# Summing two halves of each attention head in the store, moving two loads to another queue, and scaling the last rows in place

## The chip, the cores and the metric

The kernel is written in a tile framework for one Trainium2 chip and runs on one core of it. The core has TensorE for matrix products, VectorE (DVE), ScalarE (ACT) and GpSimd (POOL) for elementwise work, and SyncE (SP), which here only issues transfers. SP, ScalarE and GpSimd each have a queue for transfers (DMA) between the chip's memory (DRAM) and the on-chip buffer. The metric is the time of one execution on the device, in microseconds; the time given is the median of several runs.

The author writes the instructions in a program order and names tiles out of pools with a fixed number of buffers. A planner then decides in which order each engine takes its own instructions and which buffer a tile gets, and adds the waits on semaphores that the data need. On the chip each engine works through its list strictly in order: an instruction whose inputs aren't there holds back all that stand behind it on that engine, issues of transfers included.

## What is computed

One decoder block over 1024 tokens of width 1024, in float32: a norm, one wide projection, two token mixers, a gated merge, an output projection, and a gated FFN with a short convolution, then a last norm.

```python
xn = rms_norm(h, norm_mix_g)
proj = xn @ w_in                       # q, k, v of both mixers, gates
o_sb  = stick_breaking_attention(...)  # 8 heads of 64, causal
o_gla = gla_chunked(...)               # 4 heads, gated linear attention in chunks
y = sigmoid(gate_sb + b0) * (o_sb @ w_branch_sb) + sigmoid(gate_gla + b1) * (o_gla @ w_branch_gla)
h = h + y @ w_out
h = h + conv_ffn(rms_norm(h, norm_ffn_g))
return rms_norm(h, norm_final_g)
```

The change concerns the way `o_sb` takes from the attention to its product with `w_branch_sb`, the loads of keys for the gated linear attention ("the gated branch"), and the very last rows that are written.

## The kernel before

**Split products.** A float32 value is used on TensorE as a high and a low part: `split(h, l, src)` (L121) rounds `src` into `h` on ScalarE (L122, a cast) and subtracts on VectorE (L113) to get `l`. `mac` (L199) multiplies high by high, high by low and low by high into one bank of PSUM; its matmuls are those of line 205.

**Attention** (`attend`, L883). The eight heads are taken in four pairs `j`; in each pair `tp` counts four steps of two blocks of 128 queries, and `e` the two heads. For every chunk of up to four blocks of keys, `weigh` (L821) computes scores on TensorE (L828), a sigmoid on ScalarE (L830) and a scan on VectorE (L833, L835) into a tile `ke` of the pool `t2`. Up to `AHEAD` = 6 chunks are in flight; then `turn_weights` transposes them on TensorE (L842) and splits them. When both blocks of a step are turned, `gather` (L865) multiplies them with the values (L871). Keys and queries of the next pair come through the POOL queue (`keys`, `queries`, L737).

The values stand in a tile as 64 columns of high parts beside 64 columns of low parts. So the bank that `gather` fills has 128 rows: rows 0 to 63 hold the head's result from the high parts, rows 64 to 127 that from the low parts, and the head's output is the sum of the two. `gather` adds a bias (L877, ScalarE) into a tile `o` of pool `t2` and stores each half of `o` on its own, through SP (L879): the first to rows `head * 64` on of the scratch matrix `osb_d`, the second to the same rows further down by 512.

`heads(th)` (L847) brings this back for one half `th` of the sequence: for each of four groups of 128 rows it loads the two matrices' parts into two `t2` tiles (SP, L855), adds them (VectorE, L119) and splits the sum (L122, L113) into `ob[th]`, from which `branch(0, ...)` (L1072) multiplies with `w_branch_sb`. `heads(0)` is stepped along inside `attend` once head 7 has finished step `tp` = 1; `heads(1)` follows at the start of the gated branch (L1161).

**Gates beside it.** Pieces of the merge-gate projection (`gates`, L686) are mixed into attention as filler for TensorE; they end in a sigmoid (L719) and a store in ScalarE's queue (L720).

**After attention.** `branch(0, ...)` first loads four slabs of `w_branch_sb` (L181; two of the loads through POOL, L1077); then `fetch_rest` (L956) loads the two tiles `kt` of keys for the gated branch through POOL (L962). The gated branch (`gated`, L1047) starts with `states`, whose matmuls (L970) read `kt`; TensorE alternates between it and `branch(0, ...)`. Its `out_pair` copies a bank on ScalarE (L998), masks it on POOL (L999) and multiplies (L1007).

**Pools.** `t2` has 11 buffers of 128x512, `t4` 14 of 128x1024, `t8` 16 of 128x2048, and there are 8 banks.

**The end.** The last phase of the FFN's product ends four times in `fourth_done` (L1417), for rows of the second half of the sequence: subtract the bank, square and sum, root and reciprocal, scale both halves of the row by the norm's factor and by `norm_final_g`. The scaled row is put into one of two `spare` tiles, which `third_done` (L1402) used before, and stored through POOL; the very last one goes out in two halves through SP and ScalarE.

Of the kernel before, what the change touches and what calls it, by code (L numbers as in the profile page):

```python
# [12 lines left out]
AF = mybir.ActivationFunctionType  # L13
ALU = mybir.AluOpType
# [3 lines left out]
P = 128  # L18
# [4 lines left out]
HALF = 512  # L23
# [45 lines left out]
def block_kernel(ctx: ExitStack, tc: tile.TileContext, x, norm_mix_g, w_in, b_gate, w_alpha_up, b_alpha,  # L69
                 gla_norm_g, w_branch_sb, w_branch_gla, w_out, norm_ffn_g, w_ffn_in, conv_w, conv_b,  # L70
                 w_ffn_out, norm_final_g, out):
    nc = tc.nc
    x, out = x[0], out[0]
# [6 lines left out]
    def nm(s):  # L80
        uid[0] += 1
        return f"{s}_{uid[0]}"
# [7 lines left out]
    def t8(dt=F32R):  # L90
        return sb.tile([P, 2 * D], dt, tag="t8", name=nm("t8"), bufs=16)

    def t4(dt=F32):
        return sb.tile([P, D], dt, tag="t4", name=nm("t4"), bufs=T4)

    def t2(dt=F32):
        return sb.tile([P, HALF], dt, tag="t2", name=nm("t2"), bufs=T2)

    def bank():
        return ps.tile([P, HALF], F32, tag="bank", name=nm("bank"), bufs=8)  # L100

    def dram(name, rows, cols, dt=F32):
        return dp.tile([rows, cols], dt, tag=name, name=name)

    def by(a, k):
        return a.rearrange("p (k c) -> p k c", k=k)

    def quarter():

        return [by(t8(), 4) for _ in range(2)]  # L110

    def sub(o, a, b):
        nc.vector.tensor_tensor(out=o, in0=a, in1=b, op=ALU.subtract)  # L113
# [4 lines left out]
    def add(o, a, b):  # L118
        nc.vector.tensor_tensor(out=o, in0=a, in1=b, op=ALU.add)  # L119

    def split(h, l, src):  # L121
        nc.scalar.copy(h, src)  # L122
        sub(l, src, h.bitcast(F32))
# [43 lines left out]
    qd_d, ki_d, kt_d = (dram(n, GH * GK, S) for n in ("qd_d", "ki_d", "kt_d"))  # L167
    gate_d, ga_d = dram("gate_d", 2 * D, S), dram("ga_d", 2 * RANK, S)
    osb_d = dram("osb_d", 2 * SBH * SBD, S)
# [388 lines left out]
    for half in range(2):  # L558
# [5 lines left out]
        o = t2()  # L564
# [162 lines left out]
    HALVES = slice(0, 64), slice(64, 128)  # L727
# [117 lines left out]
    ob, first_heads = [], []  # L845

    def heads(th):  # L847

        ob.append(quarter())
        asked, added = deque(), deque()  # L850
        for k in range(6):
            if k < 4:
                asked.append((t2(), t2()))
                for n, v in enumerate(asked[-1]):
                    nc.sync.dma_start(v, osb_d[n * HALF + k * P:n * HALF + (k + 1) * P, th * HALF:(th + 1) * HALF])  # L855
            yield
            if k > 1:
                split(*(a[:, k - 2] for a in ob[th]), added.popleft())
            if k in range(1, 5):
                a, b = asked.popleft()  # L860
                add(a, a, b)
                added.append(a)
            yield

    def gather(head, tp, ah, al):  # L865
        po = bank()
        nb = 2 * tp + 2
        for b in range(nb):
            c0 = 0 if b < nb - 1 else P
            for n, a in enumerate((ah, al)):  # L870
                nc.tensor.matmul(po[:, c0:2 * P], vt[b][:, head, :], a[b // 4][:, b % 4, c0:],  # L871
                                 start=(b == 0 and n == 0), stop=(b == nb - 1 and n == 1))
        o = t2()[:, 0:2 * P]
        for n in range(2):
            c = slice(n * P, (n + 1) * P)
            i = head * NT + 2 * tp + n
            nc.scalar.activation(o[:, c], po[:, c], AF.Identity, bias=vend[:, i:i + 1])  # L877
        for n, r in enumerate(HALVES):
            nc.sync.dma_start(osb_d[n * HALF + head * 64:n * HALF + (head + 1) * 64, tp * 2 * P:(tp + 1) * 2 * P], o[r])  # L879
        if head == SBH - 1 and tp == 1:  # L880
            first_heads.append(heads(0))

    def attend():  # L883
# [10 lines left out]
        for j in range(SBH // 2):  # L894
            t, nxt = nxt, []
            for tp in range(NT // 2):
# [5 lines left out]
                for e in range(2):  # L902
                    ng = (2 * tp + 2 + 3) // 4
                    ah, al = ([by(t4(F32R), 4) for _ in range(ng)] for _ in range(2))
                    for ii in range(2):
                        i = 2 * tp + ii
                        nb = i + 1
                        right = None
                        for b0, b1 in ([(0, nb)] if nb <= 4 else [(4, nb), (0, 4)]):
                            while len(todo) == AHEAD or sum(d[1] for d in todo) > BLOCKS:  # L910
                                if len(late) > LATE:
                                    gather(*late.popleft())
                                flush()
                            right = weigh(t, e, i, b0, b1, right)
                            if j == 0:
                                chunk += 1
                                if chunk in HOLD:
                                    hold(right)
                                if chunk == AGAIN:
                                    whole21()  # L920
                                if chunk >= 2:
                                    fill(gate_steps, MORE * (chunk < 8))
                                    value_blocks(2 * tp + 2)
                            g = b0 // 4
                            d = [a[g][:, 0:b1 - b0, ii * P:(ii + 1) * P] for a in (ah, al)]
                            end = (2 * j + e, tp, ah, al) if ii == 1 and b0 == 0 else None
                            todo.append((right, b1 - b0, *d, end))
                            for v in first_heads:
                                next(v, None)
                            yield b1 - b0  # L930
        while todo:
            flush()
            while late:
                gather(*late.popleft())
            for v in first_heads:
                next(v, None)
            yield 2
# [18 lines left out]
    def fetch_rest():  # L956

        small = [by(t2(), 4) for _ in range(2)]
        state.extend((v[:, 0], v[:, 1]) for v in small)
        for p in range(2):  # L960
            kt = t4()
            nc.gpsimd.dma_start(kt, kt_d[p * P:(p + 1) * P, :])  # L962
            gla[p] += by(kt, NT), by(t4(), NT)

    def states(p, n0, n1):
# [186 lines left out]
    first_branch = branch(0, ob, w_branch_sb)  # L1152
    fill(first_branch, 1)
    fetch_rest()
    fill(gate_steps, 128)
    xq.clear()
    og = [quarter() for _ in range(2)]
    n = 0
    for _ in gated():
        if n == HEADS_AT:  # L1160
            fill(heads(1), 12)  # L1161
        n += 1
        fill(first_branch, n % GLA[1] < GLA[0])
        pace(0)
# [119 lines left out]
    acts, hr = [], []  # L1284
# [44 lines left out]
    def row(i, j):  # L1329
        return hr[i][:, j * HALF:(j + 1) * HALF]  # L1330
# [57 lines left out]
    gfin = []  # L1388
# [26 lines left out]
            mul(row(4 + i, 1), row(4 + i, 1), gfin[0][:, HALF:])  # L1415

    def fourth_done(i, p4):  # L1417
        r = row(4 + i, 0)
        sub(r, r, p4)
        o = spare[i % 2]  # L1420
        a, b = ss[i]
        nc.scalar.activation(o[:, :HALF], r, AF.Square, accum_out=b)
        add(a, a, b)
        nc.scalar.activation(b, a, AF.Sqrt, bias=eps, scale=1.0 / D)
        nc.vector.reciprocal(a, b)
        nc.scalar.activation(o[:, HALF:], row(4 + i, 1), AF.Copy, scale=a)
        nc.vector.scalar_tensor_tensor(out=o[:, :HALF], in0=r, scalar=a, in1=gfin[0][:, :HALF],
                                       op0=ALU.mult, op1=ALU.mult)
        t = slice((4 + i) * P, (5 + i) * P)
        if i < 3:  # L1430
            nc.gpsimd.dma_start(out[t, :], o)
        else:
            nc.sync.dma_start(out[t, :HALF], o[:, :HALF])
            nc.scalar.dma_start(out[t, HALF:], o[:, HALF:])

    for n, _ in enumerate(jobs):
        if n == 0:
# [9 lines left out]
    spare = [t4() for _ in range(2)]  # L1447
    spare8 = by(t8(F32), 4)
    phase(first, 2, 0, first_done, residual)
    phase(second, 2, 0, second_done, last_norm)  # L1450
    phase(third, 2, TILED[0], third_done)
    phase(fourth, 1, TILED[1], fourth_done, squares)


# [25 lines left out]
```

## Time and profile before

| | |
|---|---|
| median of 3 runs | 1386.93 us (1386.27 to 1387.03) |
| the profiled execution, its own time | 1386.67 us |
| its span, first to last instruction | 1384.8 us |
| instructions | 18329 |
| mean granted TensorE clock | 0.997 |
| read from and written to DRAM | 160.28 MB, 66.45 MB |

The profile lists for each engine the time in which it worked, and for each group of instructions what ended the idle time ahead of it. A row names the line of the kernel, the engine, the operation, the tiles (output<-input) and their shapes. Many instructions come from helpers: L113 is any subtraction, L119 any addition, L122 any cast of a split, L205 any product by `mac`, L181 any load by `load`. Such lines are told apart by their place in time. In a timeline, rows are start, duration, engine, line, operation, and in brackets how long the engine stood idle before and what ended that; "SPq", "ACTq" and "POOL ... DMA_DIRECT2D" are issues of transfers. "To landing" is the time from the issue to the end of a transfer.

Attention lies at about 343 to 538 us of the span, the gated branch with `branch(0, ...)` at 538 to 600, and the last matmul ends at 1377.6.

### The profile page before, as it was taken

Reading aid. Unit: us, or ns where it says so; the run is one execution under the profiler, and the core shown is the slowest. Engines: PE = TensorE matmul, PEld = TensorE weight load, DVE = VectorE, ACT = ScalarE, POOL = GpSimd, SP = SyncE. Lnnn points to the kernel's source line nnn. Section 1 sums busy time; section 2 is a strip of 40 time slices with the busy share of each in tenths; the row PEclk is TensorE's granted clock in tenths of the full one; section 3 lists DMA queues with packets and bytes.
Section 4 is the critical chain, followed back from the end, with each engine's and each line's share of the span. In section 5 each row is a group of like instructions: output and inputs, shape, how many; then the busy total and the mean of one; then the engine's idle time right before and its main releaser. Section 6 shows DMA issues by size and latency. Waiting matters only on the chain.

```text
span 1384.8 us, 18329 instructions
## 1 busy us (share of the span) xinstructions
PE 1372.4 (99%) x6559; PEld 1138.8 (82%) x6559; DVE 1064.6 (77%) x1640; ACT 643.9 (46%) x1244; POOL 136.3 (10%) x233
## 2 busy tenths in 40 slices
PE   9999999999999999999999999999999999999997
PEld 6788888888888888888888788888888888888886
DVE  6388688874878877658348998998888977896765
ACT  7334445653766664724126443343333334454654
POOL 2002123101111002200000000000000000000000
PEclk9999999999999999999999999999999999999999
DMA  6335278448776567673325245554444537953332
GB/s 239 132 117 151 84 221 251 143 158 210 216 158 151 131 197 237 198 237 136 136 91 177 52 120 187 196 189 152 150 163 152 182 107 272 322 163 102 99 101 105
DMA packets 164108, 227.92 MB, mean 165 GB/s; under 512 B 10938, under 2 KB 105276, under 8 KB 163506
## 3 DMA queue, kind: packets, MB, share of 16 engines
q1 hardware_dynamic: 134944, 139.01, 33.0%
q0 software_dynamic: 22496, 73.73, 16.8%
q10 hardware_dynamic: 6578, 14.03, 2.7%
q8 instruction: 51, 0.84, 0.3%
q14 instruction: 39, 0.32, 0.1%
HBM read 160.28 MB, written 66.45 MB: 164 GB/s over the span
## 4 chain that ended last, share of the span: by engine, by line
PE 95%; DVE 3%; ACT 1%; issue 0%; DMA 0%; ACTq 0%; DVEq 0%
PE bank L205 58%; PE bank L1343 15%; PE bank L385 6%; PE bank L1210 6%; PE bank L871 3%; PE bank L828 2%; PE bank L842 2%; DVE t L113 2%; PE bank L494 1%; PE bank L340 1%; DVE t L119 1%; PE bank L562 1%; PE bank L1007 1%; PE bank L970 0%; PE bank L994 0%
## 5 line engine op out<-in xcount | busy, mean ns | idle before, releaser
L205 PE MATMUL bank<-t,t 128*128 128x512 f32 x3624 | 861.1, 393 | 0.9 <-DVE t L113 0.7
L205 PEld LDWEIGHTS bank<-t,t 128*128 128x128 f32 x3624 | 676.5, 188 | 143.1 <-DVE t L113 1.6
L113 DVE TENSOR_TENSOR t<-t,t 128x512 fp32r<-128x512 f32 (+3 forms) x655 | 434.6, 697 | 93.5 <-ACT t L122 87.2
L122 ACT CAST t<-t 128x512 fp32r<-128x512 f32 (+1 forms) x543 | 320.3, 627 | 325.4 <-DVE t L113 81.0
L119 DVE TENSOR_TENSOR t<-bank,t 128x512 f32<-128x512 f32 x266 | 179.3, 685 | 97.9 <-PE bank L205 54.9
L1343 PE MATMUL bank<-t,t 128*128 128x512 f32 x924 | 209.6, 389 | 0.0
L1343 PEld LDWEIGHTS bank<-t,t 128*128 128x128 f32 x924 | 173.5, 188 | 36.0
L113 DVE TENSOR_TENSOR t<-bank,t 128x512 fp32r<-128x512 f32 (+4 forms) x124 | 69.5, 574 | 27.5 <-ACT t L122 26.9
L1210 PE MATMUL bank<-t,t 128*128 128x512 f32 x384 | 88.8, 391 | 0.0
L1241 ACT ACTIVATE t<-t,vcol 128x1024 f32<-128x1024 f32 x22 | 27.4, 1245 | 127.5 <-DVE t L119 127.5
L113 DVE TENSOR_TENSOR t<-t 128x512 f32<-128x512 f32 x120 | 83.3, 701 | 4.1 <-DMA t<-in_w_ffn_in_dram 3.7
L1210 PEld LDWEIGHTS bank<-t,t 128*128 128x128 f32 x384 | 71.6, 188 | 14.6
L119 DVE TENSOR_TENSOR t<-t,t 128x512 f32<-128x512 f32 x115 | 75.5, 686 | 9.8 <-ACT t L628 8.6
L122 ACT CAST t<-bank 128x512 fp32r<-128x512 f32 (+3 forms) x120 | 60.3, 512 | 48.8 <-PE bank L842 26.8
L385 PE MATMUL bank<-t,t 128*128 128x512 f32 x336 | 77.9, 391 | 0.0
L385 PEld LDWEIGHTS bank<-t,t 128*128 128x128 f32 x336 | 62.7, 188 | 13.1 <-DVE t L113 0.2
L1243 DVE SCALAR_TENSOR_TENSOR t<-t,vcol,t 128x1023 f32<-128x1023 f32 (+1 forms) x44 | 56.3, 1279 | 14.1 <-ACT t L1241 13.9
L833 DVE TENSOR_TENSOR_SCAN t<-t,t 128x128 f32<-128x128 f32 (+1 forms) x64 | 51.6, 816 | 17.5 <-ACT t L830 17.2
L828 PE MATMUL bank<-t,t 128*128 128x128 f32 (+3 forms) x192 | 54.6, 369 | 0.0
L842 PE MATMUL bank<-ident,t 128*128 128x128 f32 x288 | 53.2, 273 | 0.0
L871 PE MATMUL bank<-t,t 128*128 128x256 f32 (+1 forms) x320 | 51.0, 276 | 1.2 <-ACT t L122 0.7
L830 ACT ACTIVATE t<-bank 128x128 f32<-128x128 f32 (+3 forms) x96 | 46.9, 507 | 7.2 <-DMA osb_d<-t 3.2
(164 smaller groups left out, 813.5 us busy)
## 6 DMA issues: line engine op xcount, KB each, us to landing
t<-in_w_ffn_in_dram SPq DMA_DIRECT2D x50, 512.0 KB, 5.1
t<-in_w_in_dram SPq DMA_DIRECT2D x43, 512.0 KB, 5.3
act_d<-t POOLq DMA_DIRECT2D x22, 512.0 KB, 5.8
t<-in_w_ffn_out_dram SPq DMA_DIRECT2D x22, 512.0 KB, 7.6
wsum_d<-t POOLq DMA_DIRECT2D x22, 512.0 KB, 4.5
t<-act_d SPq DMA_DIRECT2D x22, 512.0 KB, 5.9
t<-wsum_d SPq DMA_DIRECT2D x44, 256.0 KB, 3.1
t<-in_w_ffn_out_dram SPq DMA_DIRECT2D x33, 256.0 KB, 2.7
```

The costliest lines, as they stand in the source:

```text
L113: nc.vector.tensor_tensor(out=o, in0=a, in1=b, op=ALU.subtract)
L119: nc.vector.tensor_tensor(out=o, in0=a, in1=b, op=ALU.add)
L122: nc.scalar.copy(h, src)
L205: nc.tensor.matmul(pt, a[:, kk], b[:, kk], start=start and kk == 0 and m == 0, stop=stop and kk == k - 1 and m == 2)
L385: nc.tensor.matmul(pt, a[:, k % 4, t], b, start=k == 0 and m == 0, stop=k == NK - 1 and m == 2)
L828: nc.tensor.matmul(z[:, 0:w], q[:, a, e, ts_], kk[:, e, b0 * P:b1 * P], start=a == 0, stop=a == 1)
L833: nc.vector.tensor_tensor_scan(out=kr, data0=kr, data1=above[:, 0:w], initial=1.0, op0=ALU.mult, op1=ALU.max)
L842: nc.tensor.transpose(pt[:, b * P:(b + 1) * P], ke[:, b * P:(b + 1) * P], ident)
L871: nc.tensor.matmul(po[:, c0:2 * P], vt[b][:, head, :], a[b // 4][:, b % 4, c0:], start=(b == 0 and n == 0), stop=(b == nb - 1 and n == 1))
L1210: nc.tensor.matmul(pt, a[:, k % 4, t], b, start=(k == 0 and m == 0), stop=(k == NK - 1 and m == 2))
L1243: nc.vector.scalar_tensor_tensor(out=cv[:, i:], in0=av[:, :S - i], scalar=col(V_CW, (2 - i) * NF + f), in1=cv[:, i:], op0=ALU.mult, op1=AL ...
L1343: nc.tensor.matmul(pts[m][i], a[:, t], b, start=(k == 0 and x_ == 0), stop=(k == NH - 1 and x_ == 2))
```

## The change

Three things are changed.

First, `gather` still stores the first half of `o` through SP, but the second half goes through POOL's queue to the same rows, as a transfer that adds to what stands there (`accum_op=ALU.add`). `heads` then loads one tile for each group of rows instead of two, and adds nothing. The second half of `osb_d` is no longer used.

Second, `fetch_rest` issues its two loads of `kt` in ScalarE's queue instead of POOL's.

Third, `fourth_done` scales the rows in place in `hr`, its square goes to `spare8`, and the stores read `hr`.

```diff
     def heads(th):
         ob.append(quarter())
-        asked, added = deque(), deque()
+        asked = deque()
         for k in range(6):
             if k < 4:
-                asked.append((t2(), t2()))
-                for n, v in enumerate(asked[-1]):
-                    nc.sync.dma_start(v, osb_d[n * HALF + k * P:n * HALF + (k + 1) * P, th * HALF:(th + 1) * HALF])
+                asked.append(t2())
+                nc.sync.dma_start(asked[-1], osb_d[k * P:(k + 1) * P, th * HALF:(th + 1) * HALF])
             yield
             if k > 1:
-                split(*(a[:, k - 2] for a in ob[th]), added.popleft())
-            if k in range(1, 5):
-                a, b = asked.popleft()
-                add(a, a, b)
-                added.append(a)
+                split(*(a[:, k - 2] for a in ob[th]), asked.popleft())
             yield
@@ gather
-        for n, r in enumerate(HALVES):
-            nc.sync.dma_start(osb_d[n * HALF + head * 64:n * HALF + (head + 1) * 64, tp * 2 * P:(tp + 1) * 2 * P], o[r])
+        dst = osb_d[head * 64:(head + 1) * 64, tp * 2 * P:(tp + 1) * 2 * P]
+        nc.sync.dma_start(dst, o[HALVES[0]])
+        nc.gpsimd.dma_start(dst, o[HALVES[1]], accum_op=ALU.add)
@@ fetch_rest
-            nc.gpsimd.dma_start(kt, kt_d[p * P:(p + 1) * P, :])
+            nc.scalar.dma_start(kt, kt_d[p * P:(p + 1) * P, :])
@@ fourth_done
-        r = row(4 + i, 0)
+        r, q = row(4 + i, 0), row(4 + i, 1)
         sub(r, r, p4)
-        o = spare[i % 2]
         a, b = ss[i]
-        nc.scalar.activation(o[:, :HALF], r, AF.Square, accum_out=b)
+        nc.scalar.activation(spare8[:, i], r, AF.Square, accum_out=b)
         add(a, a, b)
         nc.scalar.activation(b, a, AF.Sqrt, bias=eps, scale=1.0 / D)
         nc.vector.reciprocal(a, b)
-        nc.scalar.activation(o[:, HALF:], row(4 + i, 1), AF.Copy, scale=a)
-        nc.vector.scalar_tensor_tensor(out=o[:, :HALF], in0=r, scalar=a, in1=gfin[0][:, :HALF],
-                                       op0=ALU.mult, op1=ALU.mult)
+        nc.scalar.activation(q, q, AF.Copy, scale=a)
+        nc.vector.scalar_tensor_tensor(out=r, in0=r, scalar=a, in1=gfin[0][:, :HALF], op0=ALU.mult, op1=ALU.mult)
         t = slice((4 + i) * P, (5 + i) * P)
         if i < 3:
-            nc.gpsimd.dma_start(out[t, :], o)
+            nc.gpsimd.dma_start(out[t, :], hr[4 + i])
         else:
-            nc.sync.dma_start(out[t, :HALF], o[:, :HALF])
-            nc.scalar.dma_start(out[t, HALF:], o[:, HALF:])
+            nc.sync.dma_start(out[t, :HALF], r)
+            nc.scalar.dma_start(out[t, HALF:], q)
```

## The prediction, made before the changed kernel was run

> **What bounds the kernel now.** I read the page's busy shares and chain of waits first, then the busy time by stages, then the timeline of each engine around the places that the change touches.
>
> ```profile
> PE 1372.4 (99%) x6559; PEld 1138.8 (82%) x6559; DVE 1064.6 (77%) x1640; ACT 643.9 (46%) x1244; POOL 136.3 (10%) x233
> PE 95%; DVE 3%; ACT 1%; issue 0%; DMA 0%; ACTq 0%; DVEq 0%
> L205 PE MATMUL bank<-t,t 128*128 128x512 f32 x3624 | 861.1, 393 | 0.9 <-DVE t L113 0.7
> ```
>
> TensorE is busy in 1372.4 of 1384.8 us, and 95% of the chain that ended last is TensorE. So an edit that takes work from another engine pays only where TensorE stands still: 12.4 us in all. The view by stages says where these are (the columns are length, then busy time and count of PE, PEld, DVE, ACT and POOL, then clock and DMA):
>
> ```profile
> 500.00:540.00 40.00, 38.76 (x225) 33.03 (x224) 28.86 (x42) 22.83 (x51) 2.63 (x4) 1.00 0.61 185
> 733.00:772.00 39.00, 38.15 (x183) 30.87 (x181) 38.36 (x63) 25.20 (x48) 1.60 (x3) 1.00 0.57 162
> 1377.60:1384.80 7.20, 0.00 (x0) 0.00 (x0) 1.76 (x4) 1.74 (x4) 0.53 (x1) 0.70 0.38 146
> ```
>
> That is 1.24 us at the end of attention, 0.85 in the turn to the FFN and 7.20 after the last matmul; the rest of the 12.4, 3.1, lies at the start. The change works in attention, in what follows it and in the last blocks, so 1.24 us and the last 7.20 are all that it can reach directly. The 1.24 us are two waits:
>
> ```profile
> 525.24 0.38 PE L871 MATMUL bank<-t,t 128*128 128x256 f32 x1 [0.53 <-DVE t L113]
> 532.06 0.39 PE L871 MATMUL bank<-t,t 128*128 128x256 f32 x1 [0.71 <-ACT t L122]
> ```
>
> **The change, part by part. The adds.** The eight adds of `heads` go (four for each half of the sequence).
>
> ```profile
> L119 DVE TENSOR_TENSOR t<-t,t x8: 669/682/693, 513.9 to 550.0; 128x512 f32<-128x512 f32 x8
> 526.75 1.28 DVE L119 TENSOR_TENSOR t<-t,t 128x512 f32<-128x512 f32 x2
> 527.46 1.22 ACT L122 CAST t<-t 128x512 fp32r<-128x512 f32 x2 [4.21 <-DVE t L119]
> 530.44 1.57 ACT L122 CAST t<-bank 128x512 fp32r<-128x512 f32 x3
> ```
>
> 8 x 0.682 = 5.5 us leave VectorE. Only those beside the two waits can count. ScalarE stood 4.21 us for the pair at 526.75, and behind that cast stood the casts of 530.44 for which TensorE waited 0.71 us at 532.06. I take that 0.71 as gained. The 0.53 at 525.24 ends a run of scans and subtractions on VectorE, with idle time between it and the earlier adds; I take nothing of it. So this term is -0.7, with ends 0 (the cast waits for its load instead) and -1.24 (both waits go).
>
> **The stores.** 32 issues on SP become 32 accumulating issues on POOL, and 8 loads on SP go.
>
> ```profile
> osb_d<-t SPq DMA_DIRECT2D x64, 64.0 KB, 4.4
> t<-osb_d SPq DMA_DIRECT2D x16, 256.0 KB, 4.1
> dv_d<-t POOLq DMA_DIRECT2D x9, 256.0 KB, 2.4
> t<-sqkl_d POOLq DMA_DIRECT2D x24, 256.0 KB, 6.7
> 428.26 1.17 POOL L737 DMA_DIRECT2D t<-sqkh_d  x2 [25.21 <-PE bank L828]
> ```
>
> The last row has two POOL issues in 1.17 us, about 0.6 each, so 32 cost some 19 us of an engine that is 10% busy. The path is touched only through waits. Every accumulate has to wait until the plain store of the same rows has landed (4.4 us from its issue), and POOL takes its instructions in order, so everything behind it waits too. No row shows an accumulating transfer. I bound its landing by the quickest and the slowest frequent POOL transfers above, 2.4 and 6.7 us, and use 4.4, the row of the same shape. From a store's issue to a complete sum it is then 4.4 + 0.6 + 4.4 = 9.4 us (7.4 to 11.7) instead of 4.4.
>
> Who waits for that? First `heads(0)`: it needs the stores of tp 0 and 1, and the first row here is the last of these (the four stores behind it are those of tp 2 and 3 of the last two heads); the second group of its loads follows:
>
> ```profile
> 506.68 1.09 SPq L879 DMA_DIRECT2D osb_d<-t  x2
> 521.31 1.96 SPq L855 DMA_DIRECT2D t<-osb_d  x4
> 530.07 7.04 SPq L879 DMA_DIRECT2D osb_d<-t  x6
> 536.02 1.08 SPq L879 DMA_DIRECT2D osb_d<-t  x2
> ```
>
> 506.68 + 9.4 = 516.1 (518.4 at worst), before the second group of loads at 521.31: no cost. Then `heads(1)`, which needs the very last store: 536.02 + 9.4 = 545.4 (543.4 to 547.7), then its load 4.1 and its split, 0.62 + 0.69 us:
>
> ```profile
> 550.76 0.62 ACT L122 CAST t<-t 128x512 fp32r<-128x512 f32 x1 [1.44 <-DVE t L119]
> 551.28 1.06 ACT L998 COPY t<-bank 128x512 f32<-128x512 f32 x2
> 559.91 1.66 PE L205 MATMUL bank<-t,t 128*128 128x512 f32 x6
> ```
>
> Its cast can begin at 549.5 (547.5 to 551.8), against 550.76 now, and the product that reads it is the one at 559.91. Direct slack is at least 6 us. What stands behind the cast on ScalarE is the copy of L998, the mask's input, so at the worst end 1.0 us comes through there. I take 0. On SP, the gate loads and branch weights stand behind the last of these loads now as well; with half the loads and half the t2 tiles it isn't reached later.
>
> **Behind the accumulates on POOL** stand the fetches of keys and queries, then the first branch weights.
>
> ```profile
> POOL t L737 <- PE bank L828: 83.5, 5, 25.3
> 443.38 1.19 POOL L737 DMA_DIRECT2D t<-sqkh_d  x2 [10.71 <-PE bank L828]
> 526.20 0.77 POOL L181 DMA_DIRECT2D t<-in_w_branch_sb_dram  x1 [35.08 <-issue]
> 538.40 0.69 ACT L719 ACTIVATE t<-bank,vcol 128x512 f32<-128x512 f32 x1 [2.40 <-PE bank L205]
> 538.44 1.75 PE L205 MATMUL bank<-t,t 128*128 128x512 f32 x6
> t<-in_w_branch_sb_dram POOLq DMA_DIRECT2D x2, 512.0 KB, 4.5
> ```
>
> The fetches wait for room, not for POOL: the group at 428.26 is first read after the pair of heads ends, at 443.38 or later. 443.38 - 428.26 - 2.4 (its issues) - 6.7 (landing) = 6 us of slack, against one wait for a store of 4.4: no cost. The branch weights are the tight case. The gate's last product is over at 538.40 (its sigmoid starts), so the matmuls at 538.44 are the branch's first. Their weights must have landed 1.3 us before (the split), so the load must be issued by 538.44 - 1.3 - 4.5 = 532.6; now it is at 526.20, 6.4 us earlier. Whether an accumulate of the late stores (from 530.07) stands ahead of it is a matter of the planned order, which I price below. In the forecast it stands behind them: 0.
>
> **The keys of the gated branch.**
>
> ```profile
> 528.82 1.17 POOL L962 DMA_DIRECT2D t<-kt_d  x2 [0.36 <-PE bank L871]
> 538.20 0.59 PE L970 MATMUL bank<-t,t 128*128 128x256 f32 x2
> t<-kt_d POOLq DMA_DIRECT2D x2, 512.0 KB, 6.3
> 529.30 0.33 ACTq L720 DMA_DIRECT2D gate_d<-t  x1
> ```
>
> On ScalarE the two issues cost 2 x 0.33 = 0.66 us, and they wait there, in order, for tiles that gather's matmuls release. Ahead of the casts of 530.44 this is on the path: 0 to +0.66 for the issue. If they are passed only at 533.1, behind the casts that end there, the keys land at 537.5 (4.4) to 539.4 (6.3), and L970 stands up to 1.2 us. Together 0 to +1.9; the queue is otherwise waiting for TensorE in much of these us, so I take +0.3.
>
> **The last blocks.** In place of `spare` the same instructions of the same sizes write `hr`. What the edit removes is the wait of a square for the store that reads `spare[i % 2]`.
>
> ```profile
> 1374.31 0.53 POOL L1431 DMA_DIRECT2D out_dram<-t  x1 [2.87 <-DVE t L1427]
> 1378.34 0.63 ACT L1422 ACTIVATE t<-t 128x512 f32<-128x512 f32 x1 [1.20 <-DVE t L113]
> out_dram<-t POOLq DMA_DIRECT2D x7, 512.0 KB, 2.9
> ```
>
> That store lands at 1374.31 + 2.9 = 1377.2, before its tile is written at 1378.34, and the row names VectorE as what ended the wait. So nothing is removed: 0.
>
> **The sum** is -0.7 + 0.3 = -0.4. The profiled execution took 1386.67 us (1.87 more than its span); it becomes 1386.3. The median shown, 1386.93, is 0.26 above it, so the forecast is 1386.5, and with the ends of the terms (-1.24 to +1.9 + 1.0) 1385.7 to 1389.8.
>
> **The rivals.** Slower first: **the branch weights behind an accumulate**. As the text is written, the accumulates of all gathers come before these loads. Behind the store at 530.07 the load would be issued at 530.07 + 4.4 + 0.6 = 535.1, 2.5 us past the point of 532.6; behind the one at 536.02 at 541.0, 8.4 us past it. The branch's first matmul is late by that, and TensorE has nothing else in its order: middle +5.4, 1392.3. For it speaks that a plan made with quicker transfers than the chip's would put them that close. Against it: the load waits for a gather's matmuls only, which is earlier than that gather's store, and engines here don't keep the written order (gather and gate matmuls alternate one by one). The Trainium skill, "DMA: Bandwidth & Descriptors", in its section on the anatomy of one DMA on the gpsimd path, has the rule behind this: a DMA's semaphore wait is held by the issuing sequencer and not by the DMA engines. By that rule, the 35.08 us before the load at 526.20 is such a held wait, and the trace agrees. The same section's fit (2.0 us plus bytes over 436e3 per us) would give an estimate of 2.15 us for each 64 KB transfer, so 4.9 instead of 9.4 us for the chain; the row of 4.4 us speaks against so little.
>
> **Too few t2 tiles.** The tile of a gather is held through both transfers.
>
> ```profile
> L830 ACT ACTIVATE t<-bank x96: 258/568/681, 345.3 to 522.2; 128x512 f32<-128x512 f32 x48, 128x128 f32<-128x128 f32 x16, 128x256 f32<-128x256 f32 x16, 128x384 f32<-128x384 f32 x16
> ...
>   DMA osb_d<-t: 3.2, 4
> ```
>
> That is L830, the sigmoid of the scores, which has already waited four times (3.2 us) for a store that held its tile. Each hold grows by 0.6 + 4.4 = 5.0 us. TensorE works up to 6 chunks ahead, at 177 us for 96 chunks some 11 us, which hides one such wait; if one in the four isn't hidden it costs +5, 1391.9.
>
> **Nothing is gained**: the adds are hidden, and the casts then wait for their loads. 1386.9.
>
> **Faster than the idle time allows.** A busy TensorE is not at its peak:
>
> ```profile
> L205 PE MATMUL bank<-t,t 128*128 128x512 f32 x78 | 23.0, 404 | 0.0
> ```
>
> From 505 to 540 a matmul of L205 takes 404 ns, against 393 on the whole. If VectorE's relief brought back 78 x 11 ns = 0.9 us, both waits (1.24) and, by another order, the 0.85 of the later stage, it would be -3.0: 1383.9.
>
> **Chances.** Forecast 0.50, branch weights 0.17, t2 tiles 0.13, faster 0.12, nothing gained 0.08. About 0.2% (2.8 us) is what a measurement of this kernel can tell from no change. So faster 0.12, same 0.58, slower 0.30. The range reaches from 1384.0 to 1392.5: it has the forecast and nothing gained, most of the branch weights' case and half of the t2 tiles' lighter one, and leaves out the heavier ends of both and most of the faster case. The likeliest case alone is 1385.7 to 1389.8.
>
> **What would show it.** Right: L119 has eight instructions fewer, TensorE's idle time between 500 and 560 is under 1.5 us, the branch loads of POOL are issued before 532.6, and the last 7.2 us have the same rows. Wrong: an idle stretch of TensorE before the branch's first L205 or before L970 with a DMA behind it, or ScalarE's L830 waiting for osb_d in far more than four places, would mean a rival; a gain above 2.8 us would mean that the busy rows of attention hid waits that I couldn't see.

## The result, and the profile after

The changed kernel takes 1397.26 us (median; 1396.65 to 1397.56). The kernel before, run beside it, took 1386.95. The ratio is 1.0075 (95% interval 1.0057 to 1.0092): 10.3 us slower, outside the range of 1384.0 to 1392.5. The profiled execution took 1397.56 us, its span is 1395.6, 10.8 more than before.

The page of the changed kernel, busy time and chain:

```profile
PE 1375.3 (99%) x6559; PEld 1140.0 (82%) x6559; DVE 1057.8 (76%) x1632; ACT 643.8 (46%) x1244; POOL 163.3 (12%) x263
PE 95%; DVE 3%; DMA 1%; ACT 1%; issue 0%; DVEq 0%; ACTq 0%
```

VectorE has its eight instructions less (1632 for 1640). In the chain a DMA now has 1%, where it had 0%. Its name is in the view of the waits (engine, tile and line that waited <- what ended it: us in total, times, longest):

```profile
PE bank L966 <- DMA t<-kt_d: 7.2, 1, 7.2
...
PE bank L828 <- ACT t L830: 0.4, 1, 0.4
PE bank L842 <- DVE t L113: 0.3, 1, 0.3
```

L966 is the line that was L970, the first matmul of the gated branch. It waits for the keys. TensorE's timeline there, and then ScalarE's:

```profile
535.11 3.19 PE L205 MATMUL bank<-t,t 128*128 128x512 f32 x13
545.48 1.19 PE L966 MATMUL bank<-t,t 128*128 128x256 f32 x2 [7.17 <-DMA t<-kt_d]
```

```profile
531.80 1.19 ACT L122 CAST t<-t 128x512 fp32r<-128x512 f32 x2
535.31 0.62 ACT L872 ACTIVATE t<-bank,t 128x128 f32<-128x128 f32 x2 [2.32 <-PE bank L866]
538.34 0.69 ACT L719 ACTIVATE t<-bank,vcol 128x512 f32<-128x512 f32 x1 [2.40 <-PE bank L205]
538.77 0.33 ACTq L958 DMA_DIRECT2D t<-kt_d  x1
538.92 0.61 ACT L122 CAST t<-t 128x512 fp32r<-128x512 f32 x1
539.13 0.45 ACTq L958 DMA_DIRECT2D t<-kt_d  x1
```

What counts is the order. The keys' loads (L958, once L962) stand behind the last gate's sigmoid, L719. That instruction waits until TensorE has finished the gate's last product. The next thing on TensorE is the matmul that reads the keys. So the load can't leave before the moment in which its data are wanted: 538.77 instead of 528.82 on POOL, and it lands some 7 us later (t<-kt_d, the view of the DMA issues; the row of the accumulating stores is used further down):

```profile
osb_d<-t POOLq DMA_DIRECT2D x32, 64.0 KB, 2.8
...
t<-kt_d ACTq DMA_DIRECT2D x2, 512.0 KB, 7.1
```

Behind the wait TensorE is slow for a while. The busy time by windows (columns as in the prediction's view by stages; the number behind the five engines is the granted clock):

```profile
538.00:542.00 4.00, 0.30 (x2) 0.00 (x0) 1.29 (x2) 1.71 (x3) 0.83 (x1) 1.00 0.89 259
542.00:546.00 4.00, 0.52 (x1) 0.50 (x2) 0.00 (x0) 1.85 (x3) 0.00 (x0) 0.53 0.98 322
546.00:550.00 4.00, 4.00 (x13) 3.19 (x12) 0.88 (x4) 0.62 (x1) 0.37 (x1) 0.62 0.66 220
550.00:554.00 4.00, 4.00 (x20) 3.31 (x19) 2.94 (x7) 0.25 (x1) 1.61 (x3) 1.00 0.81 258
```

The clock falls to half during the wait. A mean of 0.62 over 546 to 550 is half speed until 549.0, so from 545.48 on 3.5 us of matmuls ran at half speed: 1.8 us lost. The Trainium skill, "TensorE: Matmul & The Clock Gate", Part 1, has the rule: after about 3.4 us of idle time the array gets half its clock, and full clock again after about as long of work. The trace agrees here (7.17 us idle, 3.5 us until full speed). The experiments below differ: there it took 4.8 to 6.2 us of work until full speed, and in one an idle stretch of 2.82 us was enough.

One more cost lies at the very end. POOL's closing DRAIN (duration min/median/max in ns, first and last start), before and then after:

```profile
L1476 POOLq DRAIN  x3: 46/93/6346, 1377.7 to 1384.5; - x3
```

```profile
L1470 POOLq DRAIN  x3: 46/97/8139, 1386.7 to 1395.3; - x3
```

Counted along the span, as after minus before:

| landmark | before | after | lag |
|---|---|---|---|
| first matmul that reads the keys (L970, L966) | 538.20 | 545.48 | +7.28 |
| L1210, L1206, first matmul of the FFN | 653.1 | 662.1 | +9.0 |
| last output store issued on SP | 1380.59 | 1389.57 | +8.98 |
| end of the span | 1384.8 | 1395.6 | +10.8 |

So the 10.8 us are 7.3 of wait, 1.7 more by 662 us (the half clock), nothing between 662 and 1389, and 1.8 of a longer drain.

### The profile page after: what moved, and what is told of

The parts are those of the page before. It is cut to its first block, busy times and chain, and to the rows that moved or that the text cites. A ratio compares the mean times of both kernels' runs of the same rounds, so it can differ in the third digit from the quotient of the medians.

```text
span 1395.6 us, 18306 instructions
## 1 busy us (share of the span) xinstructions
PE 1375.3 (99%) x6559; PEld 1140.0 (82%) x6559; DVE 1057.8 (76%) x1632; ACT 643.8 (46%) x1244; POOL 163.3 (12%) x263
## 4 chain that ended last, share of the span: by engine, by line
PE 95%; DVE 3%; DMA 1%; ACT 1%; issue 0%; DVEq 0%; ACTq 0%
PE bank L205 58%; PE bank L1339 15%; PE bank L385 5%; PE bank L1206 5%; PE bank L866 3%; PE bank L828 2%; PE bank L842 2%; DVE t L113 2%; PE bank L340 1%; DVE t L119 1%; PE bank L562 1%; PE bank L1003 1%; PE bank L494 1%; PE bank L966 0%; DMA t<-kt_d 0%
## 5 line engine op out<-in xcount | busy, mean ns | idle before, releaser
L1206 PE MATMUL bank<-t,t 128*128 128x512 f32 x384 | 88.8, 391 | 0.0
L1206 PEld LDWEIGHTS bank<-t,t 128*128 128x128 f32 x384 | 71.6, 188 | 14.6
L119 DVE TENSOR_TENSOR t<-t,t 128x512 f32<-128x512 f32 x107 | 70.0, 684 | 9.4 <-ACT t L628 8.6
L1243 POOL DMA_DIRECT2D act_d<-t x22 | 11.7, 532 | 352.2 <-DVE t L116 352.2
L830 ACT ACTIVATE t<-bank 128x128 f32<-128x128 f32 (+3 forms) x96 | 47.2, 509 | 9.2 <-DMA osb_d<-t 2.7
```

The lines of the kernel that those rows point to most:

```text
L830: nc.scalar.activation(ke[:, 0:w], z[:, 0:w], AF.Sigmoid, scale=-SBD ** -0.5)
L1206: nc.tensor.matmul(pt, a[:, k % 4, t], b, start=(k == 0 and m == 0), stop=(k == NK - 1 and m == 2))
```

## The experiments

Theory A: the cost is the place of the keys' load in its queue's list, in ScalarE's queue and, with accumulating stores, in POOL's also. The rivals: the accumulating stores themselves hold up the gated branch, or the in-place blocks cost at the end. No kernel here leaves out work. "Lag" is the issue of the last output store against 1380.59 of the kernel before.

| kernel | median, us | ratio (95%) | wait before the keys' matmul | lag | drain |
|---|---|---|---|---|---|
| before | 1386.7 to 1386.95 | 1 | none | 0 | 6.35 |
| changed | 1397.26 | 1.0075 (1.0057 to 1.0092) | 7.17 | 8.98 | 8.14 |
| 1 keys back on POOL | 1398.84 | 1.0091 (1.0074 to 1.0108) | 8.73 | 10.76 | 8.30 |
| 2 only the keys moved | 1396.58 | 1.0071 (1.0056 to 1.0086) | 7.21 | 9.75 | 6.18 |
| 3 only in place | 1386.75 | 1.0001 (0.9991 to 1.001) | none | 0.17 | 6.35 |
| 4 keys on SP, late | 1393.36 | 1.0045 (1.003 to 1.006) | 2.82 | 5.29 | 8.14 |
| 5 plain stores on POOL | 1396.28 | 1.0068 (1.0052 to 1.0083) | 4.90 | 7.84 | 8.14 |
| 6 keys early on SP | 1391.67 | 1.0032 (1.002 to 1.0045) | none | 1.16 | 8.14 |
| 7 as 6, drain early | 1388.81 | 1.0015 (1.0006 to 1.0024) | none | 1.28 | 7.90 |
| 8 before, drain early | 1386.51 | 0.9998 (0.9989 to 1.0007) | none | 0.11 | 6.10 |
| 9 as 7, accumulates first | 1386.30 | 1.0001 (0.9993 to 1.001) | none | -0.30 | 7.90 |
| 10 keys early on POOL | 1386.43 | 1.0003 (0.9994 to 1.0012) | none | -0.15 | 8.06 |
| 11 as 9, copies first | 1385.34 | 0.9989 (0.998 to 0.9998) | none | -0.80 | 7.90 |

### 1. The changed kernel with the keys back in POOL's queue

```diff
-            nc.scalar.dma_start(kt, kt_d[p * P:(p + 1) * P, :])
+            nc.gpsimd.dma_start(kt, kt_d[p * P:(p + 1) * P, :])
```

> The changed kernel with the two loads of kt back in POOL's queue; TensorE's, VectorE's and SP's lists are the same as in the changed kernel. Theory A (what counts is where a load stands in its queue): in POOL's list the loads now stand behind the accumulate of the last gather, which was issued at 539.5 us, so they go out at about 540.4, even later than the 538.8 on ScalarE; TensorE stands 8 to 9 us before the first matmul of the gated branch, and the kernel takes 1398 to 1400. Rival B (ScalarE's queue is what is slow): about 1388.

It is no better: 1398.84. POOL's timeline and TensorE's:

```profile
537.71 0.83 POOL L875 DMA_DIRECT2D osb_d<-t  x1 [3.82 <-DMA osb_d<-t]
538.26 1.42 POOL L958 DMA_DIRECT2D t<-kt_d  x2
```

```profile
545.95 1.22 PE L966 MATMUL bank<-t,t 128*128 128x256 f32 x2 [8.73 <-DMA t<-kt_d]
```

The keys stand behind the last accumulating store, which waits until the plain store of the same rows has landed. They go out about as late as on ScalarE (538.26 against 538.77). With accumulating stores POOL's place is lost too, so the two parts of the change can't simply be parted by undoing one.

### 2. The kernel before with the keys' move alone

The diff is the one above the other way round: L962 from gpsimd to scalar, nothing else.

> The kernel before with only the two loads of kt moved to ScalarE's queue; all other lists are those of before. Theory A: the loads go out behind the last gate's sigmoid at about 538.8 instead of 528.8, TensorE stands some 7 us before the gated branch and then works some 4 us at half clock: +8.5 to +9.5, so 1395.5 to 1396.5, and the end of the kernel is as before. Rival C (the accumulating stores slow everything around them and the load's place alone does little): +0 to +2, 1387 to 1389.

1396.58 us: the move alone costs nearly all of it, a wait of 7.2 us and 2.4 us of half clock behind it. TensorE waits as in the changed kernel, with no accumulating store there:

```profile
545.64 1.19 PE L970 MATMUL bank<-t,t 128*128 128x256 f32 x2 [7.21 <-DMA t<-kt_d]
```

### 3. The kernel before with the last blocks in place

Only the part of the diff in `fourth_done`.

> The kernel before with only the last blocks scaled in place. Theory A: no difference, 1387.0 within 0.7, and the time between the last issue and the end of the span stays at 4.2 us. Rival D (the 1.8 us more between the last issue and the end of the span, 6.0 against 4.2, come from the in-place stores): +1.8, 1388.7.

1386.75 us, ratio 1.0001 (0.9991 to 1.001), and the drain is 6.35 us as before. This part does nothing, and the longer drain isn't from it.

### 4. The changed kernel with the keys on SP

```diff
-            nc.scalar.dma_start(kt, kt_d[p * P:(p + 1) * P, :])
+            nc.sync.dma_start(kt, kt_d[p * P:(p + 1) * P, :])
```

> The changed kernel with the loads of kt on SP, where they stand behind the plain store of the last gather (issued at 536.0); the lists of TensorE, VectorE and POOL are the same. Theory A: they go out at about 536.5, 2.3 us before those on ScalarE, and TensorE stands 3 to 5.5 us: 1392 to 1396. Rival C: no better than the changed kernel, 1397.

SP issues them behind the last plain store, at 535.95, 2.8 us sooner than ScalarE did, and TensorE waits 2.82 us instead of 7.17:

```profile
540.59 1.19 PE L966 MATMUL bank<-t,t 128*128 128x256 f32 x2 [2.82 <-DMA t<-kt_d]
```

```profile
538.00:542.00 4.00, 1.42 (x3) 1.17 (x4) 1.48 (x3) 1.51 (x3) 0.83 (x1) 0.72 0.88 261
542.00:546.00 4.00, 4.00 (x11) 3.15 (x10) 0.97 (x4) 1.14 (x2) 0.37 (x1) 0.50 0.89 302
546.00:550.00 4.00, 4.00 (x18) 3.30 (x17) 2.38 (x6) 1.33 (x3) 1.62 (x3) 0.93 0.67 197
```

The wait shrank by 4.35 us and the lag by only 3.7. A clock of 0.93 over 546 to 550 is half speed until 546.6, so the matmuls from 540.59 on lost 3.0 us, more than the wait itself. Here measurement and rule differ: that page of the Trainium skill gives an idle stretch of about 3.4 us, and 2.82 were enough. What besides the length of a wait decides whether the clock falls, no run here shows.

### 5. The kernel before with plain stores through POOL

```diff
-            nc.sync.dma_start(osb_d[n * HALF + head * 64:..., ...], o[r])
+            (nc.gpsimd if n else nc.sync).dma_start(osb_d[n * HALF + head * 64:..., ...], o[r])
```

> Kernel before, with one edit: the stores of the heads' second halves go through POOL's queue as plain stores; the adds of the halves, the in-place blocks and the keys' place (POOL) are as before. The planner's POOL list then has the keys' two loads behind the last of these stores. Theory A (the keys' load passes only when the instruction ahead of it in its queue has passed): the last store waits for ScalarE's L877 of the last piece, done near 536.0, so the keys go out near 537 and L970 waits 4 to 6 us; with some 2 us of half clock behind it the kernel takes 1392 to 1395. Rival B (it is the accumulation that spoils POOL's place, not the queue): no wait before L970, 1386 to 1388. POOL's closing DRAIN: if it grows with the number of POOL's DMAs, 8.1 us as after; if it grows with accumulation alone, 6.3 as before.

```profile
537.85 0.55 POOL L879 DMA_DIRECT2D osb_d<-t  x1 [4.67 <-ACT t L877]
538.39 1.11 POOL L962 DMA_DIRECT2D t<-kt_d  x2
```

```profile
543.41 1.22 PE L970 MATMUL bank<-t,t 128*128 128x256 f32 x2 [4.90 <-DMA t<-kt_d]
```

No accumulation, and the keys go out as late (538.39 against 538.26 in kernel 1): accumulation isn't needed for the loss. A late plain store ahead of them in POOL's list does it as well. The wait is shorter than in kernel 1 because TensorE stopped 1.3 us later and the loads landed in 6.2 us, not 8.0. Without any accumulating store they took 8.6 in kernel 2, so that difference isn't the accumulation's; its cause stays open. The time, 1396.28, is above the 1392 to 1395 expected, since the store itself went out only at 537.85. The drain of 8.14 us shows that it goes by transfers on POOL, not by accumulation.

### 6. The changed kernel with the keys ahead of SP's last two stores

```diff
-        nc.sync.dma_start(dst, o[HALVES[0]])
-        nc.gpsimd.dma_start(dst, o[HALVES[1]], accum_op=ALU.add)
+        stores.append((nc.sync.dma_start(dst, o[HALVES[0]]), nc.gpsimd.dma_start(dst, o[HALVES[1]], accum_op=ALU.add)))
...
-            nc.scalar.dma_start(kt, kt_d[p * P:(p + 1) * P, :])
+            m = nc.sync.dma_start(kt, kt_d[p * P:(p + 1) * P, :])
+            for v in stores[-2:]:
+                after(v[0], m)
```

`after(b, a)` binds the planner to put `a` ahead of `b`; it adds no work.

> Changed kernel, with the keys' two loads in SP's queue ahead of the last two plain stores of the heads; the other engines' lists are those of the changed kernel. Theory A: the keys go out at 529 to 531 and land before 538.2, L970 waits for nothing, the half clock is gone, and what is left against the kernel before is POOL's longer closing drain (+1.8) and whatever the accumulating stores cost or gain: 1387 to 1389.5. If instead the accumulating stores themselves hold the gated branch up (their landing of up to 7 us, the second heads' load behind it), 1391 or more.

The keys go out at 529.55, their matmul waits for nothing, and the lag falls from 8.98 to 1.16. But 1391.67 is above the expected 1389.5, and a new wait of 2.0 us stands on TensorE. The lists weren't quite those of the changed kernel: on POOL the planner had put an operation of the gated branch (L978) ahead of the last two accumulating stores. POOL's timeline, and the chain's later steps in SP's, ScalarE's and TensorE's:

```profile
540.62 0.37 POOL L978 TENSOR_SCALAR t<-t,emid 128x128 f32<-128x128 f32 x1 [7.52 <-ACT t L122]
541.06 1.71 POOL L874 DMA_DIRECT2D osb_d<-t  x2
```

```profile
536.13 8.79 SPq L854 DMA_DIRECT2D t<-osb_d  x4
544.98 0.90 SPq L1090 DMA_DIRECT2D t<-gate_d  x2
546.32 0.93 SPq L181 DMA_DIRECT2D t<-in_w_branch_sb_dram  x2
```

```profile
552.12 1.14 ACT L122 CAST t<-t 128x512 fp32r<-128x512 f32 x2 [4.26 <-DVE t L976]
553.17 1.06 ACT L995 COPY t<-bank 128x512 f32<-128x512 f32 x2
```

```profile
554.62 1.16 PE L1004 MATMUL bank<-t,t 128*128 128x128 f32 x8 [1.97 <-POOL t L996]
```

The sums are complete only when these accumulates land. SP's last load of the second heads (L854) waits for them, the branch weights (L181) stand behind that load, ScalarE's casts wait for the weights (546.3 + 5.7 of landing = 552.0; the row names VectorE, which had long been done), and the copy that the mask and L1004 need stands behind the casts. So the other case of the expectation, accumulating stores that hold up the gated branch, came about too, in part. The runs of this kernel spread from 1389.73, the profiled one, to 1393.11; what the slower ones wait for isn't in a profile and stays open.

### 7. As 6, with the drain early

```diff
-            nc.gpsimd.dma_start(out[t, :], hr[4 + i])
+            nc.sync.dma_start(out[t, :], hr[4 + i])
```

> As the previous kernel, and the first three output stores of the last stage go through SP's queue instead of POOL's, so that POOL's last DMA is some 20 us earlier and its closing drain can run beside the last output blocks. Theory A with the drain as a cost at the end: the drain is over before the last output store lands, the end is that store's landing (3 us after its issue), and the kernel takes 2 to 3 us less than the previous one: 1385 to 1387. If the drain begins only when every engine is done, or isn't what ends last: no difference.

1388.81 us, 2.9 less than kernel 6 by the medians and 1.8 less by the profiled spans (1387.8 and 1386.0), with a lag 0.12 greater. POOL's last transfer is at 1356.1, and its drain of 7.90 us no longer ends the kernel. The 1.8 us at the end of the changed kernel are thus the drain.

### 8. The kernel before, with the drain early

The same edit at L1431 of the kernel before.

> Kernel before, with the first three output stores of the last stage in SP's queue instead of POOL's. If POOL's drain is counted from its last DMA and ends last: the drain (over at 1384.1) goes and the last store's landing near 1383.3 remains, 0.5 to 1 us less than before: 1386.0 to 1386.5. If the drain isn't what ends the kernel: 1386.9, no difference.

0.3 us less by the medians, ratio 0.9998 (0.9989 to 1.0007): not to be told from no change. Before, the drain ends at 1384.1 and the last store lands at 1383.3 (1380.6 + 2.7). So taking the drain away gains little, 0.8 us at most, while a drain longer by 1.8 us ends last with all of that.

### 9. As 7, with the last accumulating stores ahead of the branch's first operation

```diff
-            nc.gpsimd.tensor_scalar(out=sm[:, n + 1, :], in0=new, ...)
+            m = nc.gpsimd.tensor_scalar(out=sm[:, n + 1, :], in0=new, ...)
+            if n == n0 == 0:
+                after(m, stores[-1][1])
```

> As the kernel with the keys early in SP's queue and the first three output stores on SP, and POOL's last two accumulating stores stand again ahead of the gated branch's first operation on POOL (in that kernel the planner had put one such operation ahead of them, and they went out at 541 instead of 532 and 539). Theory C (the 2.0 to 2.3 us wait at the first causal product of the gated branch came from these late accumulating stores, through SP's load of the second heads and the branch weights queued behind it, and ScalarE's cast of these weights): the last accumulate goes out near 538.5, the branch weights near 543, the wait goes, and the kernel takes 2 to 2.5 us less than that one: 1386 to 1387, the time of the kernel before within 0.1%. If the wait comes from somewhere else (the branch weights' own landing): 1388 to 1389.

1386.30 us, within 0.1% of before, as Theory C had it. The accumulates go out at 535.15 and 537.04 and the branch weights at 544.38. The wait at the first causal product doesn't go entirely; it falls from 2.33 (kernel 7) to 1.13:

```profile
553.17 1.16 PE L1006 MATMUL bank<-t,t 128*128 128x128 f32 x8 [1.13 <-POOL t L998]
```

```profile
550.67 1.14 ACT L122 CAST t<-t 128x512 fp32r<-128x512 f32 x2 [4.82 <-DMA t<-in_w_branch_sb_dram]
551.72 1.07 ACT L997 COPY t<-bank 128x512 f32<-128x512 f32 x2
```

### 10. The changed kernel with the keys early on POOL, drain early

```diff
-            nc.scalar.dma_start(kt, kt_d[p * P:(p + 1) * P, :])
+            m = nc.gpsimd.dma_start(kt, kt_d[p * P:(p + 1) * P, :])
+            for v in stores[-3:]:
+                after(v[1], m)
```

`stores` and the edit of the drain are those of kernels 6 and 7.

> Changed kernel with the keys' two loads in POOL's queue ahead of the last three accumulating stores, which puts them behind the second load of branch weights alone, and with the first three output stores on SP. Theory A: the keys go out when that load has passed, at 532 to 533.5, and land near 539.5, so L966 waits 0.5 to 2.5 us, less than half of the 8.7 us that it waited with the keys behind the last accumulate; 1387 to 1390. If POOL's queue is bad for the keys wherever they stand in it: 7 us or more before L966 and 1394 or more.

```profile
527.10 0.78 POOL L181 DMA_DIRECT2D t<-in_w_branch_sb_dram  x1 [2.83 <-PE bank L205]
528.22 1.09 POOL L957 DMA_DIRECT2D t<-kt_d  x2 [0.34 <-PE bank L866]
533.91 0.86 POOL L874 DMA_DIRECT2D osb_d<-t  x1 [4.61 <-DMA osb_d<-t]
```

Better than expected: without an accumulate ahead of it the second load of branch weights passes at 527.10, not 532, so the keys leave at 528.22 and no wait is left there. In the queue in which kernel 1 waited 8.73 us, three places earlier, the keys cost nothing. With kernels 1, 2 and 5 this shows Theory A: the place in the list, not the queue, decides.

### 11. As 9, with ScalarE's copies ahead of its casts

```diff
+    copies = []
     def split(h, l, src):
-        nc.scalar.copy(h, src)
+        m = nc.scalar.copy(h, src)
+        if len(copies) == 2:
+            for v in copies:
+                after(m, v)
...
-            nc.scalar.copy(a, by(pa, 4))
+            copies.append(nc.scalar.copy(a, by(pa, 4)))
```

> As the kernel with the accumulates first (keys early on SP, three output stores on SP), and ScalarE's two copies of the first causal scores stand ahead of its casts of the branch weights, as they did in the kernel before. Theory C: the last wait that the accumulating stores leave, 1.13 us of TensorE at the first product behind these scores, goes, and nothing takes its place: about 1.1 us less than that kernel, 1385.2, 0.1% below the kernel before, which its interval will hardly part from no change. If the branch's products need the weights at once: the wait moves to the branch's L207 and the time stays at 1386.3.

1385.34 us, 1.0 less than kernel 9. ScalarE's timeline:

```profile
549.06 1.08 ACT L1002 COPY t<-bank 128x512 f32<-128x512 f32 x2 [1.75 <-DMA t<-gate_d]
551.88 1.14 ACT L124 CAST t<-t 128x512 fp32r<-128x512 f32 x2 [1.74 <-DMA t<-in_w_branch_sb_dram]
```

The wait of 1.13 is gone and no other took its place on TensorE behind attention. This is the one version whose whole interval lies below the kernel before, by 0.0011 (0.0002 to 0.002): of the two waits of 1.24 us that went with the adds only 0.2 is back, and what the accumulating stores push late is put back in front. Its gain is below the 0.2% that a measurement of this kernel can tell.

## Why the prediction was wrong, step by step

**The keys of the gated branch** is the step that failed. It put the issue "ahead of the casts of 530.44" or "behind the casts that end" at 533.1, took +0.3 and gave 0 to +1.9. The load stood two places further down ScalarE's list, behind L872 (once L877) and the sigmoid L719, and cost 7.2 us of wait. The row that shows what this place is worth, the sigmoid at 538.40, stood in the prediction itself, under the branch weights. From it the price could have been had: 538.8 + 6.3 = 545.1 against the 538.20 at which the keys are wanted, +6.9. For POOL's list that question was asked ("the branch weights behind an accumulate"); for ScalarE's only the two nearest places were priced. Kernel 2 shows the term alone: a lag of 9.75.

**A stall was priced one to one.** No term or rival counted the clock: each microsecond late was a microsecond. The wait cost 1.8 us on top in the changed kernel and 3.0 in kernel 4.

**The stores** were right as to the path in attention: heads(0) and heads(1) were not late by themselves, an accumulating store landed in 2.8 us (median of 32), not the 4.4 taken, and its issue cost 0.85, not 0.6. The last one took 7.0 us, so the last sum was complete at 546.5, within the 543.4 to 547.7 given. The part "19 us of an engine that is 10% busy" overlooked what those transfers do at the end: the drain, 1.8 us. No row of it was read. And "On SP, the gate loads and branch weights stand behind the last of these loads now as well" was taken at 0, with 1.0 at worst through ScalarE's copy: kernels 6, 7, 9 and 10 show 2.0, 2.3, 1.1 and 1.1 us. SP came to the branch weights no later than before (546.32 in kernel 6, 544.38 in kernel 9, 547.3 before), as the prediction had it. What it didn't price is the planner's new order on ScalarE, where the casts of these weights now stand ahead of the copy; kernel 11 shows it. In the changed kernel itself the wait for the keys hides it.

**The adds** were right: both waits went, 1.24 against the 0.7 taken. But the changed kernel had lost about as much earlier. The gate's sigmoids at 369.93 and 384.12 before are at 370.09 and 385.73 after, 1.45 us later from one to the next; the view of the waits names 0.66 of it, TensorE's two waits at 375 and 376 us. At 538.30 the gate was done at the same time as before (538.35).

**The last blocks**, 0, were right (kernel 3).

**The rivals.** Branch weights: POOL issued the loads at 524.92 and 533.72, the second behind accumulates as feared and 1.1 us past the 532.6 given. The first product of the branch shows no wait for it, but the wait for the keys would hide one. In kernels 6, 9 and 10, where the keys are in time, that load went out at 532.02, 531.45 and 527.10, and no wait came. The row of 526.20, read as a wait held on POOL, names no releaser ("issue"); two semaphore instructions of POOL at 526.2, right ahead of the load, bear the reading out.

Too few t2 tiles: by name, L830 waited for osb_d twice, 2.7 us, less than before. The page of the changed kernel:

```profile
L830 ACT ACTIVATE t<-bank 128x128 f32<-128x128 f32 (+3 forms) x96 | 47.2, 509 | 9.2 <-DMA osb_d<-t 2.7
```

The loss between 370 and 385 us is probably one more such wait, under another name:

```profile
370.34 0.86 POOL L875 DMA_DIRECT2D osb_d<-t  x1 [6.39 <-DMA osb_d<-t]
```

```profile
373.64 0.60 ACT L830 ACTIVATE t<-bank 128x512 f32<-128x512 f32 x1 [1.82 <-PE bank L205]
```

This accumulating store landed 3.2 us after its issue, at 373.5, and the sigmoid began 0.1 us later. In kernel 1 the same store went out at 369.55 and landed at 372.45, and the sigmoid began at 372.55. So the tile was most likely held through both transfers, as the rival had it, though no row names it. It cost 1.45 us, not the 5 that were priced.

"An idle stretch of TensorE ... before L970 with a DMA behind it" was named as what would show the forecast wrong, and it is just this that came. But no rival had it with a price, and the term itself went only to 1.2 us of it.

## What to carry to other kernels

When a load is moved to another queue, go down that queue's list from the first possible place to the last one before the data are wanted, and price each by the instruction ahead of it, above all by one that waits for the same engine that will want the data. A store that waits (for the store before it, or for a late producer) spoils its queue for every load behind it. Before a queue gets more transfers, look at what its engine does after the last of them. And a wait of TensorE of 2.8 us or more cost here its own length and 1.8 to 3.1 us of half clock on top.

## What the runs showed of the hardware

POOL's closing drain goes by the transfers that POOL issued. Two key loads fewer make it 0.16 us shorter (kernel 2 against before: 6.18 and 6.35), three output stores fewer 0.25 (kernel 7 against 6, kernel 8 against before): 82 ns for each transfer of 128 rows. The 32 stores of 64 rows add 1.79 as plain ones (kernel 5 against before) and 1.96 as accumulating ones (kernel 1 against before). It costs time only where POOL's last transfer is late.

Half clock came after an idle stretch of 2.82 us, and not after 1.97 and 2.33 (kernels 6 and 7, clock 1.00 in 550 to 560). The windows of 1 us in the five kernels in which the keys' matmul waits show more. "Late" is that matmul's start against 538.20, "lost" is half of the time from it to full clock.

| kernel | TensorE stops | clock falls | keys' matmul | full clock | late + lost | lag |
|---|---|---|---|---|---|---|
| changed | 538.3 | 542.2 | 545.5 | 549.0 | 7.28 + 1.78 | 8.98 |
| 1 | 537.2 | 541.9 | 546.0 | 552.1 | 7.75 + 3.08 | 10.76 |
| 2 | 538.4 | 543.6 | 545.6 | 550.4 | 7.44 + 2.40 | 9.75 |
| 4 | 537.8 | 539.8 | 540.6 | 546.6 | 2.39 + 3.00 | 5.29 |
| 5 | 538.5 | 541.9 | 543.4 | 548.7 | 5.21 + 2.65 | 7.84 |

The two terms make up the lag within 0.1 us in each of the five. The half clock came 2.0 to 5.2 us after TensorE stopped, and it lasted 6.8 us in four kernels and 10.2 in kernel 1. Of such a stretch, what doesn't fall into the wait falls into the work. So the shortest wait, 2.82 us in kernel 4, lost 3.0 us to the clock, and the 7.17 us of the changed kernel only 1.8.
